# Turning every second step of a prompt attention around: values, scores, transposes

## The chip, the cores and the metric

The kernel runs on one core of a Trainium2 chip. The time is the device time of one execution in microseconds (us). The engines named below are PE (TensorE, matrix products), PEld (its weight loads), ACT (ScalarE), DVE (VectorE), POOL (GpSimd) and SP (SyncE, which issues DMAs). The kernel before takes 1814.83 us, the median of three runs (1814.32 to 1816.25).

## The reference, cut to what matters

One layer of a hybrid decoder is computed for a prompt of 1024 tokens and 32 sample tokens. The part that the change touches is group B of the first sub-layer: causal latent attention of the prompt, with 8 heads, 96 query and key columns and 64 value columns per head.

```python
def masked_attend(q, k, v, q_pos, k_pos):
    s = jnp.einsum('...qhd,...khd->...hqk', q, k).astype(jnp.float32) * (QK_HEAD ** -0.5)
    s = jnp.where(k_pos[None, :] <= q_pos[:, None], s, NEG_INF)
    p = jax.nn.softmax(s, axis=-1).astype(v.dtype)
    return jnp.einsum('...hqk,...khd->...qhd', p, v)
```

Queries, keys and values come from normalised latents by projections (`mla_queries`, `mla_keys_values`). Around it stand a gated chunk mixer, a paged sample attention, an output projection, a memory attention and a gated feed-forward part with a causal convolution; the change leaves their code as it is.

## The kernel before, in words

All is computed in float32, mostly as three products of high and low halves (`mm3`, line 185: high by high, low by high, high by low). The stages follow each other: `phase1` (input projections, mixer), `phase2a` (prompt attention), `phase2b` (sample attention over cached pages), then output projection, memory attention and the feed-forward part.

`phase2a` cuts the attention into 16 units: a head h and a group G of four blocks of 128 queries. A unit with G = 0 (keys 0 to 511) has three steps, one with G = 1 (keys 0 to 1023) four; there are 56 steps, numbered t = 0 to 55 here. `head_unit` gives a unit its parts:

- scores `a(e)` for block e: products into a PSUM tile `s` (two buffers), which DVE moves to `pr` with the mask and the row maximum (lines 1014 and 1018), and the negative maximum `nm` (line 1020);
- exponential `e(e)` on ACT (line 1023), in place on `pr`, with the row sum;
- transposes `T(b)` (line 1031): up to four 128x128 blocks of `pr` into a PSUM tile `tp` (four buffers), which ACT copies to `pth` (line 1033);
- values `V(b)` (line 1046): products of `v` (64 columns, stationary) with `pth`, added up in the PSUM tile `o`. Even query blocks go to partitions 0 to 63 of `o`, odd ones to 64 to 127, so these products use 64 of PE's columns at a time;
- `copy` (line 1053, DVE: `oc<-o`, and a reciprocal) and `out` (line 1059: two transposes of `oc` on PE, then a scaling on DVE, lines 1063).

`head_prep` (line 984, "preps" below) transposes queries and keys of a head; `proj_group` (line 185 with an output named `tp`) makes the projections of later blocks and heads. Both use the `tp` buffers too.

The order of PE, ACT, DVE and POOL in this stage is written out by hand (`manual_schedule`): what a Python loop calls first stands first in each engine's queue. In each step of the loop the parts are called in this order: the low halves left over (`flush`), the transposes of this step with any `out` that is due, the exponentials left over from the step before (`pend`; in the last step of a unit they go ahead of the transposes), the scores of the next unit that `jobs[t]` names, the low halves and sums left over, the values of the step before, and then `extra[t]`, which holds preps, projections, norms and weight sums by a table of steps. From step 32 on, a part `sample()` of the sample attention's preparation goes one stretch further in each step; from step 50 on, so does `mix()`, which squares, scales and transposes the finished part of the output `b_all` (lines 1687, 1693, 1701).

The order of SP, and of the engines outside this stage, is set by a scheduler that the compiler front end runs on costs of its own.

## Time and profile before

| | us |
|---|---|
| median of three runs | 1814.83 (1814.32 to 1816.25) |
| the profiled execution's own time | 1815.49 |
| its span | 1813.8 |
| PE busy | 1791.1 (99%) |
| DVE busy | 1347.4 (74%) |
| ACT busy | 921.0 (51%) |
| POOL busy | 705.9 (39%) |
| prompt attention's steps, in the span | about 203 to 401 |

A row of the timeline tells the start in us from the start of the span, the duration, the engine, the line of the kernel, the operation, output and inputs by the program's names, and what an idle time before it waited for. PE's products are pipelined, so the duration of one overlaps the next; what an instruction costs is read from start to start. The granted clock of PE (PEclk) is a share of full speed. The value products show up in the timeline as two rows for each instruction.

### The profile page before, as it was taken

The page shows a single profiled execution, that of the slowest core. Times are in us where ns is not written, and L with a number is a line of the kernel's source. Part 1 is how long each engine was busy: PE and PEld are TensorE (multiplying, and loading weights), DVE is VectorE, ACT ScalarE, POOL GpSimd, SP SyncE. Part 2 cuts the span into 40 slices and gives each one's busy share as a digit, 9 for nine tenths or more (in the row PEclk, how much of TensorE's full clock was granted, in tenths as well). Part 3 has the DMA queues.
Part 4 walks back from the last instruction along what each step waited for, and adds up shares of the span by engine and source line. Part 5 has one row for each costly group of instructions (what it writes and reads, how often), then busy time and mean ns, then how long its engine had stood idle before and what let it go on. Part 6 is the DMA issues. An engine that isn't in the chain of part 4 may idle for free.

```text
span 1813.8 us, 39386 instructions
## 1 busy us (share of the span) xinstructions
PE 1791.1 (99%) x14259; PEld 1696.6 (94%) x14259; DVE 1347.4 (74%) x2778; ACT 921.0 (51%) x1931; POOL 705.9 (39%) x858
## 2 busy tenths in 40 slices
PE   9999999999999999999999999999999999999999
PEld 8999777769999999998899989999999999999999
DVE  7864777667678777787644678988888888878664
ACT  7335676766556555565434567433333333344442
POOL 1021656534455445453033001476677767400000
PEclk9999999999999999999999999999999999999999
DMA  8101354558876666663655255122222222584242
GB/s 324 48 18 62 118 184 129 164 164 229 226 206 191 190 186 194 178 190 125 188 157 195 97 169 181 58 95 83 72 71 83 72 83 83 163 319 150 88 147 78
DMA packets 153044, 261.06 MB, mean 144 GB/s; under 512 B 20881, under 2 KB 97394, under 8 KB 152850
## 3 DMA queue, kind: packets, MB, share of 16 engines
q1 hardware_dynamic: 151986, 257.50, 45.8%
q8 instruction: 113, 1.85, 0.5%
q10 hardware_dynamic: 864, 1.05, 0.2%
q14 instruction: 81, 0.66, 0.1%
HBM read 212.66 MB, written 45.82 MB: 143 GB/s over the span
## 4 chain that ended last, share of the span: by engine, by line
PE 77%; DVE 5%; ACT 2%; DMA 1%; issue 1%; POOL 1%; SPq 1%; DVEq 0%; ACTq 0%; POOLq 0%
PE s L185 22%; PE d L185 12%; PE b L185 8%; PE E L185 7%; PE F L185 7%; PE X L185 7%; PE A L185 3%; PE o L1046 2%; PE o L1537 2%; PE tp L1031 1%; PE tp L185 1%; PE s L1422 1%; PE tp L984 1%; PE v L185 1%; PE t L185 0%
## 5 line engine op out<-in xcount | busy, mean ns | idle before, releaser
L185 PE MATMUL s<-w2h,ch 128*128 128x256 f32 x1018 | 302.1, 297 | 0.0
L185 PE MATMUL s<-w2h,cl 128*128 128x256 f32 x1018 | 293.6, 288 | 0.0
L185 PE MATMUL s<-w2l,ch 128*128 128x256 f32 x1018 | 293.1, 288 | 0.0
L185 PEld LDWEIGHTS s<-w2h,ch 128*128 128x128 f32 x1018 | 191.6, 188 | 3.3 <-issue 2.9
L185 PEld LDWEIGHTS s<-w2h,cl 128*128 128x128 f32 x1018 | 191.4, 188 | 0.4 <-DVE rqa L257 0.4
L185 PEld LDWEIGHTS s<-w2l,ch 128*128 128x128 f32 x1018 | 191.8, 188 | 0.0
L1458 DVE TENSOR_REDUCE ss<-sq 128x16 f32<-128x1024 f32 x128 | 155.2, 1213 | 29.2 <-ACT sq L1455 29.1
L1407 POOL TENSOR_TENSOR cl<-cT,ch 128x512 fp32r<-128x512 f32 x64 | 86.2, 1346 | 197.8 <-ACT ch L1403 192.0
L1455 ACT ACTIVATE sq<-s 128x512 f32<-128x512 f32 x128 | 76.4, 597 | 72.3 <-PE s L185 72.2
L200 ACT CAST a<-brb 128x528 fp32r<-128x528 f32 x77 | 48.9, 634 | 114.7 <-PE d L185 111.2
L1452 ACT ACTIVATE sq<-s 128x512 f32<-128x512 f32 x128 | 76.6, 599 | 50.4 <-PE s L185 41.2
L201 DVE TENSOR_TENSOR a<-brb,a 128x528 fp32r<-128x528 f32 x77 | 54.3, 706 | 59.1 <-ACT a L200 58.8
L185 PE MATMUL d<-a,w 128*128 128x264 f32 x768 | 95.5, 285 | 1.2 <-DVE G L2366 1.2
L185 PEld LDWEIGHTS d<-a,w 128*128 128x128 f32 x768 | 94.3, 188 | 1.4 <-issue 1.4
L2233 POOL TENSOR_TENSOR lo<-s,hi 128x1024 fp32r<-128x1024 f32 x20 | 64.2, 3208 | 45.7 <-ACT hi L2232 45.7
L2289 ACT COPY a<-A 128x264 f32<-128x264 f32 x43 | 16.1, 375 | 120.6 <-PE A L185 114.3
L185 PE MATMUL mm<-wlo,xh 128*128 128x256 f32 (+3 forms) x272 | 77.1, 286 | 0.1
L185 PE MATMUL mm<-whi,xh 128*128 128x256 f32 (+3 forms) x272 | 77.1, 285 | 0.0
L185 PE MATMUL mm<-whi,xl 128*128 128x256 f32 (+3 forms) x272 | 76.9, 287 | 0.0
L1403 ACT CAST ch<-cT 128x512 fp32r<-128x512 f32 x128 | 73.6, 628 | 0.2 <-issue 0.2
L2355 POOL TENSOR_TENSOR cv<-cv,row 128x1056 f32<-128x1056 f32 x22 | 65.1, 2958 | 21.0 <-ACT cv L2354 21.0
L185 PE MATMUL d<-a,hi 128*128 128x264 f32 x552 | 72.0, 285 | 0.0
(802 smaller groups left out, 6371.3 us busy)
## 6 DMA issues: line engine op xcount, KB each, us to landing
cT<-cT SPq DMA_DIRECT2D x256, 160.0 KB, 2.7
ck<-ck SPq DMA_DIRECT2D x256, 144.0 KB, 3.5
raw<-w_up SPq DMA_DIRECT2D x44, 512.0 KB, 3.6
wsumd<-wsum SPq DMA_DIRECT2D x26, 512.0 KB, 3.5
actd<-cv SPq DMA_DIRECT2D x44, 264.0 KB, 2.4
brb<-actd SPq DMA_DIRECT2D x44, 264.0 KB, 5.6
wsum<-w_down SPq DMA_DIRECT2D x22, 512.0 KB, 3.7
raw<-wsumd SPq DMA_DIRECT2D x20, 512.0 KB, 3.7
```

The lines of the kernel that those rows point to most:

```text
L185: x = self.nc.tensor.matmul(out, l, r, start=first and i == 0, stop=last and i == len(seq) - 1)
L200: first = {"act": nc.scalar.copy, "pool": nc.gpsimd.tensor_copy, "dve": nc.vector.tensor_copy}[eng](hi, src)
L201: low = lambda: nc.vector.tensor_tensor(lo, src, hi, ALU.subtract)
L1046: nc.tensor.matmul(u["o"][g : g + 64, o : o + m * P], s["v"][:, j, h % 4], th[:, z * P : (z + m) * P], start=j == 0, stop=b == len(banks) - 1,
L1403: nc.scalar.copy(d["h"][:, k], src[k])
L1407: (nc.vector if k else nc.gpsimd).tensor_tensor(d["l"][:, k], src[k], d["h"][:, k], ALU.subtract)
L1452: nc.scalar.activation(sq[:, 0], ps[:, :, n0 : n0 + 256], AF.Square)
L1455: nc.scalar.activation(sq[:, 1], pt.rearrange("p (e d) -> p e d", e=2), AF.Square)
L1458: yield lambda: nc.vector.tensor_reduce(s["ss"][:, g0 : g0 + 2].rearrange("p e (z h) -> p z e h", z=2), sq.rearrange("p z e (h d) -> p z e ...
L1537: nc.tensor.matmul(s["o"][j * 32 : j * 32 + 32], S[:, q * 4 + j], d["ck"][:, j, :257], start=q == 0 and j > 0, stop=q == 7)
L2233: eng.tensor_tensor(lo, src, hi, ALU.subtract)
L2355: nc.gpsimd.tensor_tensor(cv, cv, row, ALU.mult)
```

## The change

Only `phase2a` is changed, in two ways.

In the odd steps the parts are called in another order: values of the step before, scores, extras, and at the end this step's transposes. In the even steps the values go from ahead of the extras to the end. So the sequence over two steps, which was transposes, scores, values, extras, and the same again, is now transposes, scores, extras, values (even), values, scores, extras, transposes (odd). The values of steps 1 and 2, of 3 and 4 and so on then stand next to each other, and so do the transposes of steps 1 and 2, 3 and 4.

In the table of extras the preps are entered after the projections, so that within a step the projections follow the scores and the preps come last. No instruction of the stage is added or taken away.

```diff
         put(split_w, (7, 8, 13, 15))
         spread(tok_s, 4, 11)
-        put(preps[1][2:], (3, 4))
-        for h in range(2, 8):
-            b = 7 * (h - 1)
-            put(preps[h], {3: (9, 10, 12, 13), 5: (27, 28, 34, 35), 6: (32, 33, 41, 42), 7: (39, 38, 44, 45)}.get(h, (b, b + 1, b + 3, b + 4)))
-        extra[2][:0] = preps[0][2:]
         spread(late[0][0], 11, 21)
...
         spread(late[2][0], 24, 30)
+        put(preps[0][2:], (2, 2))
+        put(preps[1][2:], (3, 4))
+        for h in range(2, 8):
+            b = 7 * (h - 1)
+            put(preps[h], {3: (9, 10, 12, 13), 5: (27, 28, 34, 35), 6: (32, 33, 41, 42), 7: (39, 38, 44, 45)}.get(h, (b, b + 1, b + 3, b + 4)))
...
                     self.flush()
+                    turn = [lambda b=b: u["T"](b) for b in banks] + outs.pop(t, [])
+                    values, V = V, [lambda u=u, b=b: u["V"](b) for b in banks]
                     if k == len(u["steps"]) - 1:
                         for f in pend:
                             f()
                         pend = []
-                    for b in banks:
-                        u["T"](b)
-                    for f in outs.pop(t, []):
+                    for f in values if t % 2 else turn:
                         f()
                     for f in pend:
                         f()
...
                     self.flush()
                     self.flush_sums()
-                    for f in V:
-                        f()
-                    V = [lambda u=u, b=b: u["V"](b) for b in banks]
...
                     for f in extra[t]:
                         f()
-                    t += 1
-                    if t == 32:
+                    if t == 31:
                         steps.append(sample())
                     steps = [x for x in steps if next(x, 0) is None]
+                    for f in turn if t % 2 else values:
+                        f()
+                    t += 1
```

Two places show what this does to the engines' queues. The first is PE around the last step (t = 30) of the unit h = 4, G = 0. Before, from the last score product of step 29 on (`s`), with values (`o<-pth`), transposes (`tp<-ident,pr`) and the two transposes of `out` (`tp<-ident,oc`):

```order
L185 MATMUL s_4406<-kTh_3977,qTl_4169 128x512
L1046 MATMUL o_4412<-pth_4339,v_2698 64x256 x2
L1031 MATMUL tp_4423<-ident_60,pr_749_4154 128x128
L1031 MATMUL tp_4423<-ident_60,pr_766_4233 128x128
L1059 MATMUL tp_4428<-ident_60,oc_4395 128x128 x2
L1046 MATMUL o_4412<-pth_4389,v_2698 64x128 x2
L1046 MATMUL o_4412<-pth_4389,v_2698 64x256
L1031 MATMUL tp_4443<-ident_60,pr_778_4275 128x128
```

And now, in the same place:

```order
L185 MATMUL s_4399<-kTh_3978,qTl_4183 128x512
L1030 MATMUL tp_4412<-ident_60,pr_766_4233 128x128
L1030 MATMUL tp_4412<-ident_60,pr_745_4142 128x128
L1030 MATMUL tp_4412<-ident_60,pr_736_4097 128x128
L1030 MATMUL tp_4412<-ident_60,pr_766_4233 128x128
L1030 MATMUL tp_4423<-ident_60,pr_745_4142 128x128
L1030 MATMUL tp_4423<-ident_60,pr_766_4233 128x128
L1058 MATMUL tp_4428<-ident_60,oc_4419 128x128 x2
L1045 MATMUL o_4388<-pth_4413,v_2698 64x128 x2
L1045 MATMUL o_4388<-pth_4413,v_2698 64x256
L1045 MATMUL o_4388<-pth_4424,v_2698 64x128 x2
L185 MATMUL s_4448<-kTh_4317,qTh_4377 128x128
```

The four transposes of step 29 have moved behind its scores, and the values of step 30 (`pth_4424`), which stood behind the next step's transposes and scores, now follow those of step 29 at once. In ACT's queue the copy to `pth_4424` stands behind the exponential over 1024 keys of the next unit, as it did before:

```order
L1022 ACTIVATE pr_793_4347,rsum_4274<-pr_793_4347,nm_4348,rq_2427 128x896
L1032 COPY pth_4413<-tp_4412 128x512
L1022 ACTIVATE pr_804_4392,rsum_4274<-pr_804_4392,nm_4393,rq_2427 128x1024
L1032 COPY pth_4424<-tp_4423 128x256
L1032 COPY pth_4490<-tp_4489 128x512
```

The second place is ACT at the end of the stage (from step 51 on). Before, the small copy of step 51's transposes (`pth_5533`) stood ahead of three squares of `mix()` (k, q), and two scalings of `b_all` behind that of step 55 (`pth_5624`):

```order
L1023 ACTIVATE pr_1039_5509,rsum_5425<-pr_1039_5509,nm_5510,rq_2427 128x1024
L1033 COPY pth_5533<-tp_5532 128x256
L1687 ACTIVATE k_5527,mixr_5529<-b_all_2409 128x512
L1687 ACTIVATE q_5528,mixr_5529<-b_all_2409 128x512 x2
L1033 COPY pth_5546<-tp_5545 128x512
L1033 COPY pth_5553<-tp_5552 128x512
L1033 COPY pth_5577<-tp_5576 128x512
L1033 COPY pth_5584<-tp_5583 128x512
L1033 COPY pth_5599<-tp_5598 128x512
L1033 COPY pth_5606<-tp_5605 128x512
L1693 ACTIVATE b_all_2409<-b_all_2409,mixr_5529 128x512 x2
L1033 COPY pth_5624<-tp_5623 128x256
```

Now both small copies stand behind `mix()`:

```order
L1022 ACTIVATE pr_1039_5509,rsum_5423<-pr_1039_5509,nm_5510,rq_2427 128x1024
L1686 ACTIVATE k_5523,mixr_5525<-b_all_2409 128x512
L1686 ACTIVATE q_5524,mixr_5525<-b_all_2409 128x512 x2
L1032 COPY pth_5541<-tp_5540 128x256
L1032 COPY pth_5546<-tp_5545 128x512
L1032 COPY pth_5553<-tp_5552 128x512
L1032 COPY pth_5582<-tp_5581 128x512
L1032 COPY pth_5589<-tp_5588 128x512
L1032 COPY pth_5599<-tp_5598 128x512
L1032 COPY pth_5606<-tp_5605 128x512
L1692 ACTIVATE b_all_2409<-b_all_2409,mixr_5525 128x512 x4
L1032 COPY pth_5631<-tp_5630 128x256
```

The copy of step 51 has moved behind the three squares, and the copy of step 55 behind all four scalings. On PE the values that need these two copies stand ahead of the transposes of step 53 and of `mix()`'s own transposes. Counted in PE's queue, the value products form 55 runs without another kind of product between them before, and 29 now. Outside the stage only SP's weight-sum transfers and some rows of the feed-forward part change places with a neighbour.

## The prediction

> **What bounds the kernel now.** I read the page first: PE is busy all through, so only what shortens PE's own work, or its waits, can show.

> ```profile
> PE 1791.1 (99%) x14259; PEld 1696.6 (94%) x14259; DVE 1347.4 (74%) x2778; ACT 921.0 (51%) x1931; POOL 705.9 (39%) x858
> ```

> Then the stage by itself (windows of the steps, of one stretch near their start, and of their end), who made PE wait in it, and one group of DVE's:

> ```profile
> 203.00:398.00 195.00, 186.47 (x1271) 138.44 (x1271) 132.21 (x455) 137.58 (x351) 100.77 (x151) 0.98 0.49 154
> 212.24:215.65 3.41, 2.03 (x9) 1.31 (x10) 2.15 (x5) 1.64 (x4) 0.94 (x2) 1.00 0.41 104
> 215.65:222.47 6.82, 6.82 (x26) 5.20 (x25) 4.03 (x15) 0.96 (x2) 3.10 (x5) 0.50 0.59 199
> ...
> PE tp L1031 <- ACT pr L1023: 3.0, 5, 1.1
> PE s L185 <- DVE pr L1018: 2.2, 7, 1.3
> PE tp L1031 <- DVE qTl L207: 1.1, 1, 1.1
> PE s L185 <- ACT qTh L204: 1.0, 1, 1.0
> ...
> L1053 DVE COPY oc<-o 128x256 f32<-128x256 f32 x15 | 6.2, 410 | 0.0
> ```

> After the stretch's length the columns are the busy time of PE, PEld, DVE, ACT and POOL, then the granted clock, the DMA share and GB/s. PE works 186.5 of 195 us; ACT and DVE have about 60 us to spare, but not everywhere: the waits are short and sit where ACT's exponentials or DVE's moves are late. In 215.65 to 222.47 the granted clock is 0.50, after 3.41 us in which PE was busy for 2.03 only.

> **What a run of values costs.** The timeline of PE at one step:

> ```profile
> 282.57 0.39 PE L185 MATMUL s<-kTl,qTh 96*128 96x512 f32 x1
> 282.80 0.39 PE L185 MATMUL s<-kTh,qTl 96*128 96x512 f32 x1
> 283.12 1.08 PE L1046 MATMUL o<-pth,v 128*64 128x256 f32 x8
> 284.13 0.38 PE L185 MATMUL tp<-w2h,ckh 128*128 128x256 f32 x1
> 284.36 0.28 PE L185 MATMUL tp<-w2l,ckh 128*128 128x256 f32 x1
> 284.48 0.28 PE L185 MATMUL tp<-w2h,ckl 128*128 128x256 f32 x1
> ...
> 289.05 0.66 PE L1031 MATMUL tp<-ident,pr 128*128 128x128 f32 x4
> 289.46 0.46 PE L185 MATMUL s<-kTh,qTh 96*128 96x448 f32 x1
> 289.75 0.37 PE L185 MATMUL s<-kTl,qTh 96*128 96x448 f32 x1
> 289.97 0.36 PE L185 MATMUL s<-kTh,qTl 96*128 96x448 f32 x1
> ```

> A score product takes 0.23 from start to start (282.57 to 282.80), so the values could start at 283.03; they start at 283.12, 0.09 late. Their eight rows take 1.01; the four such rows at 323.10 below take 0.58, so four rows are worth 0.43 and each run has 0.15 on top. The product behind them takes 0.23 where its neighbour takes 0.12: another 0.11; a transpose behind them loses about 0.06 (below, two at 323.68 and three at 325.06 are busy for 0.44 and 0.55, so one is 0.11, but the two take 0.28). So a run costs 0.09 + 0.15 + 0.06 to 0.11 = 0.30 to 0.35 us beside its work. Transposes between scores cost next to nothing: four and the first score product take 0.70 (289.05 to 289.75), and by themselves 4 x 0.11 + 0.22. Standing together gains nothing for them, nor does moving preps behind projections.

> The last two steps already have their values together, and show that the price is paid once:

> ```profile
> 387.19 1.08 PE L1046 MATMUL o<-pth,v 128*64 128x256 f32 x8
> 388.57 1.30 PE L1046 MATMUL o<-pth,v 128*64 128x256 f32 x10
> 389.80 0.55 PE L1031 MATMUL tp<-ident,pr 128*128 128x128 f32 x3
> ...
> 391.53 0.44 PE L1046 MATMUL o<-pth,v 128*64 128x128 f32 x4
> 391.90 1.09 PE L1031 MATMUL tp<-ident,pr 128*128 128x128 f32 x8
> 393.56 1.14 PE L1046 MATMUL o<-pth,v 128*64 128x256 f32 x8 [0.56 <-ACT pth L1033]
> 396.04 1.08 PE L1046 MATMUL o<-pth,v 128*64 128x256 f32 x8
> 397.42 1.52 PE L1046 MATMUL o<-pth,v 128*64 128x256 f32 x14
> 398.87 1.53 PE L1701 MATMUL tp<-ident,b_all 128*128 128x128 f32 x12
> 401.42 0.39 PE L1422 MATMUL s<-bd,krq 128*128 128x128 f32 x2
> ```

> Ten rows take 1.23 and four 0.37 (388.57, 391.53), together 1.60; the fourteen at 397.42 take 1.45.

> **The gain.** 26 runs fewer, at 0.09 + 0.15, are 6.2 us. What follows a run changes too: before 11 runs had a product of line 185 behind them and 44 something like a transpose (11 x 0.11 + 44 x 0.06 = 3.9); now about 23 and 6 (2.9). What scores pay behind values stands in no row; I take the 0.11 of the projection, the same kind of product, and between 0.06 and 0.16 the term moves by 1.1 either way. Sum 7.2 us, 0.28 for each pair. It counts only where PE does not wait. Nine pairs stand ahead of a wait that ACT or DVE ends: step 3 (the wait for qTh), 17, 23 (the 1.1 for qTl), 31, 41, 47, and three at the end. The other 17 give 17 x 0.28 = 4.8.

> **The price: values that now follow too soon.** Where a unit's last step is even and brings no scores, both values follow the scores of the step before almost at once. At step 30 the trace of before shows what they then wait for:

> ```profile
> 323.10 0.65 PE L1046 MATMUL o<-pth,v 128*64 128x256 f32 x4
> 323.68 0.44 PE L1031 MATMUL tp<-ident,pr 128*128 128x128 f32 x2
> 323.96 0.38 PE L1059 MATMUL tp<-ident,oc 128*128 128x128 f32 x2
> 324.27 0.86 PE L1046 MATMUL o<-pth,v 128*64 128x128 f32 x6
> 325.06 0.55 PE L1031 MATMUL tp<-ident,pr 128*128 128x128 f32 x3
> 325.93 0.77 PE L1031 MATMUL tp<-ident,pr 128*128 128x128 f32 x5 [0.32 <-ACT pr L1023]
> ...
> 324.55 1.24 ACT L1023 ACTIVATE pr<-pr,nm,rq 128x1024 f32<-128x1024 f32 x1 [0.97 <-DVE nm L1020]
> 325.79 0.35 ACT L1033 COPY pth<-tp 128x256 f32<-128x256 f32 x1
> ```

> The scores end at 323.10; the small copy is done at 326.14, 3.04 later. Before, its values came long after it. Now PE has four transposes (0.44), two more (0.22), `out` (0.31), and the values of step 29 (0.09 + 0.64, the six rows at 324.27 less 0.15) to do, 1.7 us, and then waits 1.3 for step 30's, less about 0.4 because the DVE copy to `oc` (410 ns) now stands behind the maximum. The 0.32 of before goes. So 0.6 is lost here. Behind the waiting values stand the next unit's scores, and with them DVE. Steps 16 and 40 have the same shape with projections or sample work between, and ACT has more ahead of the copy; I take 0.5 each. Sum 1.6; bounds 0 (if ACT is early) and 3.9 (three full waits of 1.3).

> **The price at the end.** ACT's rows there:

> ```profile
> 390.69 0.35 ACT L1033 COPY pth<-tp 128x256 f32<-128x256 f32 x1
> 390.94 0.63 ACT L1687 ACTIVATE k<-b_all 128x512 f32<-128x512 f32 x1
> 392.94 2.03 ACT L1033 COPY pth<-tp 128x512 f32<-128x512 f32 x4
> ```

> Without the small copy the squares run from 390.69 to 392.69, and the copy of step 51 is done at about 393.0. PE finishes step 52's transposes at 391.3 and has nothing ahead of these values: it waits 1.7 where it waited 0.56 before. Step 52's values need the second large copy (394.0) and end at 394.6; sixteen transposes and `out` follow to 396.6 (before, this point was 396.04), then eighteen value rows to 398.8. Meanwhile ACT has its last large copy out at 397.5, scales `b_all` four times (four operations of the squares' size at 0.63 are 2.5) and copies step 55 at 400.4. PE's last values and 12 transposes then start at 400.4 and 400.9; before, the 12 started at 398.87. That is 2.0 late; each pair gained before it brings all of it forward a little, so I take +1.5, with bounds of 0 and 2.5.

> **Sum.** -4.8 + 1.6 + 1.5 = -1.7 on the profiled execution's 1815.49, which is 1813.8. The three runs' median is 0.7 below that execution, part of which may be the slow clock near the start, so I forecast 1813.6. About 0.2% (3.6 us) is what a measurement of this kernel can tell from no change: under 1811.2 is faster, over 1818.5 slower.

> **Rivals.** *The waits are covered and the gain stays.* ACT has 57 us to spare in the stage; if its order happens to be early at steps 16, 30 and 40, and the tail costs nothing, 1814.8 - 7.2 = 1807.6; with half of the prices about 1810. The half clock near the start may go too: values instead of transposes now stand ahead of the wait for qTh, filling its window better, and 6.82 us at 0.50 are worth up to 3.4. Against it: the orders shown above put those copies behind long ACT work. Chance 0.27.

> *The pauses halve the clock.* At the end PE would be idle from about 389.7 to 390.7 and 391.3 to 393.0 in one window of 3.41 us, less busy than the 2.03 of 3.41 that came ahead of the half clock at 215.65. Then 6.82 us at 0.50 cost up to 3.4: 1817.0. If the pause at step 30 does the same, 1820.4, on the other side; it decides from two such drops on, or one and full waits at 16, 30 and 40. Against it: windows elsewhere in this stage have waits of 1.1 to 1.3 us without a drop. Chance of over 1818.5: 0.15. [...]

> *A run of two steps pays twice*, because its second half goes to another tile `o`. Then nothing is won and the prices stay: 1814.8 + 3.1 = 1817.9. The fourteen rows at 397.42 stay in one tile, so they do not rule it out. [...] Chance 0.05, within 0.2%.

> **Chances and range.** The forecast has 0.53 (its own range 1811.5 to 1817, from the bounds of the prices). Faster 0.27, within 0.2% 0.58, slower 0.15. The range takes in half of the first rival's case, and the second's with one drop: 1809.5 to 1818.5.

> **What would show it.** In the profile of the changed kernel: runs of values followed by scores, the first score product about 0.1 long; waits of values (line 1045) for the copy (line 1032) of 0.5 to 2 us near steps 16, 30, 40 and 52, where there was one of 0.56; the sample attention's first product (L1422) 1 to 3 us ahead of 401.42. It is wrong if values do not wait there, if the scores behind values cost far more than 0.11, or if the granted clock has more or fewer stretches at 0.50 in the stage.

## The result, and the profile after

The changed kernel takes 1824.67 us, the median of six runs (1821.92 to 1827.14), against 1815.49 (1814.32 to 1818.50) for six runs of the kernel before on the same chip: a ratio of 1.0051 (95% interval 1.0040 to 1.0061). It is slower, by about 9 us. The forecast was 1813.6 with a range up to 1818.5.

The profiled execution took 1824.68, its span 1823.0. From the page, and from the windows and PE's waits of the changed kernel, from 203 us to the sample attention's first product at 409.27 (before: 401.42):

```profile
PE 1790.2 (98%) x14259; PEld 1704.6 (94%) x14259; DVE 1348.4 (74%) x2778; ACT 919.9 (50%) x1931; POOL 706.4 (39%) x858
```

```profile
203.00:409.27 206.27, 189.82 (x1297) 149.48 (x1296) 132.82 (x460) 139.38 (x357) 102.68 (x154) 0.96 0.46 146
353.53:356.95 3.42, 1.46 (x11) 1.05 (x12) 3.24 (x14) 3.08 (x9) 1.99 (x3) 1.00 0.56 167
356.95:363.77 6.82, 6.82 (x37) 5.60 (x36) 4.21 (x14) 1.42 (x5) 4.06 (x6) 0.50 0.68 224
394.50:397.91 3.41, 1.30 (x10) 0.83 (x8) 0.13 (x1) 3.38 (x11) 0.00 (x0) 1.00 0.00 0
397.91:401.32 3.41, 3.26 (x16) 1.94 (x17) 2.10 (x13) 1.07 (x3) 0.00 (x0) 0.50 0.00 0
```

```profile
PE tp L1058 <- DVE rsum L1053: 3.3, 4, 1.6
PE tp L1030 <- ACT pr L1022: 3.1, 4, 1.2
PE tp L1030 <- DVE qTl L207: 2.9, 3, 1.4
PE o L1045 <- ACT pth L1032: 2.3, 2, 1.5
PE s L185 <- DVE pr L1017: 2.0, 7, 1.1
```

The same window and waits of the kernel before, up to 401.42:

```profile
203.00:401.42 198.42, 189.55 (x1298) 140.99 (x1296) 134.06 (x460) 140.20 (x357) 102.01 (x153) 0.98 0.48 151
```

```profile
PE tp L1059 <- DVE rsum L1054: 0.3, 1, 0.3
```

PE is idle for 206.27 - 189.82 = 16.45 us, before 198.42 - 189.55 = 8.87. Its waits for `rsum`, that is `out` waiting for DVE, went from 0.3 to 3.3; for `qTl` from 1.1 to 2.9; values for ACT's copy from 0.6 to 2.3. And the clock is at 0.50 in two stretches more, each behind a window in which PE was busy for less than half.

**An account of the stage.** For each profile I took the 1296 PE instructions (fewer or more where a kernel leaves out or adds some) up to the sample attention's first product. Idle time is the sum of the gaps before them; half clock is half of PE's busy time inside the stretches at 0.50; work is the rest. A pause that the duration of the instruction before still covers counts as work.

| | stage | idle | half clock | work |
|---|---|---|---|---|
| before | 198.5 | 8.9 | 3.4 | 186.3 |
| before, two further profiles | 198.3 / 200.0 | 8.7 / 10.0 | 3.4 / 3.4 | 186.2 / 186.6 |
| changed | 206.4 | 16.4 | 8.5 | 181.5 |
| changed, a further profile | 208.9 | 18.6 | 8.5 | 181.7 |

So the change takes 4.8 us of work off PE, adds 7.6 us of waiting, and loses 5.1 us more to the clock: 7.9 us. Split by kind of instruction, from start to start, the 4.8 are 6.4 less for values, scores, projections and preps, and 1.6 more for the transposes of `pr` and `oc`. Another 1.1 us is lost at the start of the sample attention, where a product of `cl` now waits for DVE:

```profile
PE s L1448 <- DVE cl L1406: 1.1, 1, 1.1
```

**Where it happens.** Instruction by instruction the changed kernel is mostly within 2 us of the one before from 220 to 353 us: saved work and new waits cancel. Between 353 and 360 it falls back by more than 5 us. PE and DVE around step 40:

```profile
353.68 0.87 PE L1030 MATMUL tp<-ident,pr 128*128 128x128 f32 x6 [0.96 <-DVE qTl L207]
356.12 0.41 PE L1058 MATMUL tp<-ident,oc 128*128 128x128 f32 x2 [1.57 <-DVE rsum L1053]
356.78 0.91 PE L1127 MATMUL tp<-ident,qr 32*128 32x32 f32 x8 [0.24 <-DVE kTl L201]
357.62 0.70 PE L1045 MATMUL o<-pth,v 128*64 128x128 f32 x4
```

```profile
354.64 0.75 DVE L1013 CUSTOM_DVE_ANT_0 pr<-s,cmask,nm 128x512 f32<-128x512 f32 x1
355.31 0.08 DVE L1013 DVE_READ_ACCUMULATOR2_ANT nm<- 128x1 f32 x1
355.43 0.21 DVE L1019 TENSOR_SCALAR nm<-nm,rq 128x1 f32<-128x1 f32 x1
355.56 0.41 DVE L1052 COPY oc<-o 128x256 f32<-128x256 f32 x1
355.89 0.17 DVE L1053 RECIPROCAL rsum<-rsum 128x4 f32<-128x4 f32 x1
```

Step 37 is the last of its unit and odd. Its `copy` is due two steps later, in step 39, which is odd: it is now called at that step's end, behind the score moves. Its `out` is due in step 40, which is even: at that step's start. The two have become neighbours. PE reaches `out` while DVE still moves scores, and waits 1.57 us; before, a whole step lay between. With the 0.96 ahead of it this leaves PE busy for 1.46 of 3.42 us, and 6.82 us at half clock follow.

The second loss, 4.2 us by instruction, is at the end:

```profile
395.82 0.77 PE L1030 MATMUL tp<-ident,pr 128*128 128x128 f32 x5 [0.79 <-ACT pr L1022]
398.06 2.46 PE L1045 MATMUL o<-pth,v 128*64 128x128 f32 x12 [1.47 <-ACT pth L1032]
400.46 2.37 PE L1030 MATMUL tp<-ident,pr 128*128 128x128 f32 x16
```

```profile
396.29 0.61 ACT L1686 ACTIVATE q<-b_all 128x512 f32<-128x512 f32 x1
396.81 0.19 ACT L1686 ACTIVATION_READ_ACCUMULATOR q<-b_all 128x1 f32 x1
397.03 0.63 ACT L1686 ACTIVATE q<-b_all 128x512 f32<-128x512 f32 x1
397.56 0.19 ACT L1686 ACTIVATION_READ_ACCUMULATOR q<-b_all 128x1 f32 x1
397.66 1.32 ACT L1032 COPY pth<-tp 128x256 f32<-128x256 f32 x3
```

The values wait for the copy behind the mixer's squares, as forecast, for 1.47 us; with the 0.79 before it that again leaves a window less than half busy (1.30 of 3.41), and the twelve value rows behind it and the first of the sixteen transposes run at half clock.

**What the change does give.** The values of steps 27 and 28, which go to two tiles `o`, now together, with the score product behind them:

```profile
321.23 0.87 PE L1045 MATMUL o<-pth,v 128*64 128x128 f32 x8
322.03 0.50 PE L185 MATMUL s<-kTh,qTh 96*128 96x512 f32 x1
```

Before, step 27's four rows stood here, and step 28's four at 323.10 (shown in the prediction):

```profile
319.61 0.44 PE L1046 MATMUL o<-pth,v 128*64 128x128 f32 x4
319.98 0.64 PE L984 MATMUL tp<-ident,q 128*96 128x128 f32 x4
```

Eight rows take 0.80 us from 321.23 to 322.03; before, the same eight took 0.37 and 0.58 in two places. A run that goes on in another tile `o` pays its 0.15 once. At step 30 this gain is lost:

```profile
325.43 0.41 PE L1058 MATMUL tp<-ident,oc 128*128 128x128 f32 x2 [1.08 <-DVE rsum L1053]
325.77 1.30 PE L1045 MATMUL o<-pth,v 128*64 128x128 f32 x10
327.00 0.33 PE L185 MATMUL s<-kTh,qTh 96*128 96x128 f32 x1
```

The ten rows of steps 29 and 30 take 1.23, where six and four took 0.79 and 0.37 before (at 324.27 and 327.32). ACT's copy for the last four ends at 326.58, and they start at 326.63: part of the 1.23 is a short wait.

### The profile page after: what moved, and what is told of

It is laid out like the page before. It is cut to its first block, busy times and chain, and to the rows that moved or that the text cites. A ratio compares the mean times of both kernels' runs of the same rounds, so it can differ in the third digit from the quotient of the medians.

```text
span 1823.0 us, 39392 instructions
## 1 busy us (share of the span) xinstructions
PE 1790.2 (98%) x14259; PEld 1704.6 (94%) x14259; DVE 1348.4 (74%) x2778; ACT 919.9 (50%) x1931; POOL 706.4 (39%) x858
## 4 chain that ended last, share of the span: by engine, by line
PE 75%; DVE 7%; ACT 3%; issue 2%; DMA 1%; POOL 1%; SPq 0%; DVEq 0%; ACTq 0%
PE s L185 22%; PE d L185 12%; PE b L185 7%; PE E L185 7%; PE X L185 7%; PE F L185 7%; PE A L185 3%; PE o L1045 2%; PE o L1536 2%; PE tp L1030 1%; PE tp L185 1%; PE s L1421 1%; DVE ss L1457 1%; PE v L185 1%; ACT pr L1022 1%
## 5 line engine op out<-in xcount | busy, mean ns | idle before, releaser
L185 PE MATMUL s<-w2h,ch 128*128 128x256 f32 x1018 | 302.2, 297 | 0.0
L185 PE MATMUL s<-w2h,cl 128*128 128x256 f32 x1018 | 293.9, 289 | 0.0
L185 PE MATMUL s<-w2l,ch 128*128 128x256 f32 x1018 | 293.4, 288 | 0.0
L185 PEld LDWEIGHTS s<-w2h,ch 128*128 128x128 f32 x1018 | 191.8, 188 | 3.2 <-issue 2.9
L185 PEld LDWEIGHTS s<-w2h,cl 128*128 128x128 f32 x1018 | 191.6, 188 | 0.5 <-DVE rqa L257 0.4
L185 PEld LDWEIGHTS s<-w2l,ch 128*128 128x128 f32 x1018 | 191.9, 189 | 0.0
L185 PE MATMUL d<-a,w 128*128 128x264 f32 x768 | 95.4, 285 | 1.1 <-DVE G L2365 1.1
L185 PEld LDWEIGHTS d<-a,w 128*128 128x128 f32 x768 | 94.3, 189 | 1.3 <-issue 1.3
L185 PE MATMUL mm<-wlo,xh 128*128 128x256 f32 (+3 forms) x272 | 77.2, 286 | 0.1
L185 PE MATMUL mm<-whi,xh 128*128 128x256 f32 (+3 forms) x272 | 77.2, 285 | 0.0
L185 PE MATMUL mm<-whi,xl 128*128 128x256 f32 (+3 forms) x272 | 77.0, 287 | 0.0
L2288 ACT COPY a<-A 128x264 f32<-128x264 f32 x43 | 16.1, 374 | 120.6 <-PE A L185 113.3
L185 PE MATMUL d<-a,hi 128*128 128x264 f32 x552 | 72.0, 285 | 0.0
```

The source lines that it names most:

```text
L185: x = self.nc.tensor.matmul(out, l, r, start=first and i == 0, stop=last and i == len(seq) - 1)
```

## The experiments

All are edits of the two kernels. "Idle", "half clock" and "work" are those of the account above, in the one profiled execution of each run. The longest pauses that carry a verdict are quoted; the numbers are gathered here.

| run | ratio to before (95%) | stage | idle | half clock | work |
|---|---|---|---|---|---|
| e1_outs_start | 1.0065 (1.0052 to 1.0078) | 209.2 | 20.2 | 8.9 | 180.1 |
| e2_tail_before | 1.0039 (1.0026 to 1.0052) | 204.5 | 14.2 | 8.5 | 181.7 |
| e3_filled (34 more) | 1.0037 (1.0024 to 1.0050) | 205.3 | 14.8 | 5.1 | 185.4 |
| e5_turn_only | 1.0041 (1.0029 to 1.0053) | 206.9 | 16.1 | 10.0 | 180.9 |
| e6_values_only | 1.0035 (1.0024 to 1.0046) | 205.0 | 18.3 | 7.7 | 179.0 |
| e7_values_chosen | 1.0003 (0.9993 to 1.0012) | 200.1 | 12.7 | 6.8 | 180.6 |
| e8_outs_start_sample | 1.0048 (1.0035 to 1.0061) | 210.3 | 19.0 | 10.2 | 181.1 |
| e9_values_chosen_table | 0.9998 (0.9987 to 1.0009) | 197.4 | 13.8 | 1.7 | 181.9 |
| e10_before_filled (30 more) | 1.0003 (0.9994 to 1.0012) | 196.5 | 5.9 | 0.0 | 190.6 |
| e11_outs_start_cos | 1.0023 (1.0014 to 1.0033) | 199.7 | 15.5 | 3.4 | 180.7 |
| e12_chosen_filled (38 more) | 0.9996 (0.9987 to 1.0005) | 199.3 | 11.0 | 1.7 | 186.6 |
| e13_all_filled (61 more) | 1.0034 (1.0021 to 1.0046) | 201.8 | 11.4 | 1.7 | 188.7 |
| e14_before_less (32 fewer) | 1.0008 (0.9999 to 1.0017) | 198.6 | 11.8 | 6.8 | 180.0 |

**Does `out` wait because it follows its copy too closely?** The copy and `out` go back to the step's start:

```diff
-turn = [lambda b=b: u["T"](b) for b in banks] + outs.pop(t, [])
+turn, done = [lambda b=b: u["T"](b) for b in banks], outs.pop(t, [])
-for f in values if t % 2 else turn:
+for f in (values if t % 2 else turn) + done:
```

> The changed kernel, but the copy of o and the transposes of out stand near the start of every step, behind its transposes (even) or values (odd), so that a whole step lies between a unit's copy and its out. Theory A (out waits for DVE because in units with an odd last step copy and out became neighbours): the three waits of out for line 1053's reciprocal, 3.0 us together, go, and with the pause at 356.1 us the half clock at 357 to 364, which cost 3.4; about 6.4 us less than the changed kernel, +2.8 against the kernel before (ratio 1.0015). Theory B (my prediction's step: the copy behind the row maximum helps, the values then wait instead): no gain, ratio 1.004 to 1.006, new waits of values for ACT's copies at steps 30 and 40.

The time did not fall, yet the places say more than the time. At step 40 the wait of 1.57 is gone (0.46 is left, for another reason) and no half clock follows: there theory A holds. At step 30 the wait only changed its name. The timeline of PE in this run:

```profile
325.63 0.38 PE L1058 MATMUL tp<-ident,oc 128*128 128x128 f32 x2
326.31 0.86 PE L1045 MATMUL o<-pth,v 128*64 128x128 f32 x6 [0.29 <-ACT pth L1032]
328.47 0.44 PE L1045 MATMUL o<-pth,v 128*64 128x128 f32 x4 [1.29 <-ACT pth L1032]
```

`out` no longer waits, so the values reach ACT's small copy early and wait 1.29: theory B, the prediction's own mechanism, at the 1.3 of its working. What ate the gain was new. DVE's queue at 378.76, behind it the copy, the scores and PE's `out`:

```profile
378.76 0.75 DVE L1173 TENSOR_SCALAR cosT<-cosT,cols 128x1024 f32<-128x1024 f32 x1 [4.15 <-DMA cosT<-c_cosT]
```

```profile
376.24:379.65 3.41, 1.17 (x10) 0.57 (x9) 0.89 (x2) 0.47 (x2) 1.45 (x2) 1.00 0.78 298
379.65:389.89 10.24, 7.87 (x33) 6.03 (x34) 5.24 (x18) 3.77 (x7) 0.00 (x0) 0.50 0.62 186
```

DVE waited 4.15 us for the load of `cosT`, PE 3.24 in turn, and 10.24 us at half clock followed. SP issued that load at 373.82, behind one more pair of weight-sum transfers than in the kernel before (366.40 there); that queue's order is a scheduler's. The changed kernel has that pair in front of the load too (issued at 371.78): DVE did not wait for it in the first profile, but 2.1 us in the further one, with 3.41 us at half clock behind it at 384.7. Two runs tested this, both with `copy` and `out` at the step's start. The first starts the sample preparation a step earlier (`if t == 30`), the second puts the scaling of `cosT`, and what follows it in `sample()`, two steps later (two more `yield`).

> The run with copy and out at the step's start, but the parts of the sample attention's preparation begin one step earlier, so that the load of cosT is issued about 3.5 us earlier. Theory A (in that run DVE waited 4.15 us for cosT, with out and the scores behind it, and the pause halved the clock for 10.2 us at 380): no wait for cosT, no stretch at 0.50 near 380; about 3.2 + 5.1 us less than that run, ratio 1.0015 to 1.0025. Rival (the wait at 380 comes from out itself): ratio 1.005 to 1.007 as there.

> The run with copy and out at the step's start, and DVE's scaling of cosT two steps later, so that nothing on DVE stands behind the load of cosT. Theory A (that run lost its gain at 380 us to that load, which is issued on the queue of SP after a pair of weight-sum transfers): no pause of 3.2 at 380 and no half clock there, 6 to 7 us less than that run, ratio 1.002 to 1.003. Rival (out itself waits): ratio 1.005 to 1.007.

The first missed: the load was issued only 1.7 us earlier (372.16), DVE came to it earlier still and waited 5.28, and PE 3.52. In this run 3.41 us at half clock also stood at 357.15, behind waits of 0.46 and 0.80 around step 40. The second came out as theory A expects: ratio 1.0023, no stretch at 0.50 from 376 to 391, PE busy for 13.41 of these 15 us. So the neighbours `copy` and `out` cost the changed kernel about 5 us (1.0051 against 1.0023, of which the later scaling of `cosT` may have a share), much of it through the clock, and the load of `cosT` stood ready as the next limit. Of the 5.1 us by which this profile loses less to the clock, 1.7 are not theirs: the two waits at the end were as long as in the changed kernel (0.77 and 1.47), but no half clock followed them.

**The end, and the table of extras.** One run leaves the steps from 48 on in the old order (`odd = t % 2 and t < 48`), one puts the table of extras back and keeps the turned steps.

> The changed kernel, with the steps from 48 on in the order of the kernel before. Theory A (the end lost 3.2 us through the waits at 395.8 and 398.1 and the half clock behind them, and the sample attention started 1.1 late because of it): 3 to 4 us less than the changed kernel, +5 to +6 against the kernel before (ratio 1.003), no stretch at 0.50 near 398. Theory C (the half clock there comes by its own count, whatever the waits): about 1.5 less, ratio 1.004, the stretch stays.

> The changed kernel with the table of extras in the order of before (preps ahead of the projections of their step): only the turned steps are left of the change. If the waits of transposes for DVE's low half qTl (2.9 us, before 1.1) come from preps that stand last, next to the transposes: 1 to 2 us of waits go, and the half clock at 357, whose window holds one of them (0.96), may go with them (3.4): ratio 1.002 to 1.0045. If the table is without effect: ratio 1.005, waits for qTl as in the changed kernel.

With the old end nothing more is lost after 390 us than in the kernel before (waits of 0.49 and 0.56), neither the two longer waits nor the stretch at 398 nor the 1.1 at the start of the sample attention: theory A in its places. The ratio is 1.0039, some 2 us less than the changed kernel where 3 to 4 were expected; the intervals of the two overlap. The table shows no clear effect: at 1.0041 the interval overlaps that of the changed kernel, and the waits for `qTl` stay at 2.8. With the transposes back at the start of every step (e6_values_only below) these waits fall to 1.1, as in the kernel before: they belong to the turned transposes.

**Does the clock fall because of the pauses?** Transposes of the identity, which nobody reads, ahead of `out` at steps 30 and 40 (`for _ in range(fill)`, 9 and 13), and step 52's last transpose 12 times more; then the same in more pauses of the changed kernel, where `cosT` is also scaled two steps later, and in five pauses of the kernel before.

> The changed kernel, with transposes that nobody reads in the three longest pauses of PE: 9 and 13 ahead of the transposes of out at steps 30 and 40 (1.0 and 1.4 us), 12 behind the transposes of step 52 (1.3 us). The pauses keep their length, but PE works in them. Theory A (the clock falls after a window of 3.41 us that is about half idle): the stretches at 0.50 at 357 to 364 and 398 to 401 go, 5.1 us less than the changed kernel, +4 against the kernel before (ratio 1.0023). Theory C (the drops do not hang on these pauses): same time as the changed kernel or slower, ratio 1.005, stretches still there or elsewhere.

> The changed kernel with transposes that nobody reads in seven pauses (the three of the earlier run, and ahead of transposes at steps 0, 48 and 52 and of the first scores of head 0's upper queries), and with DVE's scaling of cosT two steps later. Theory A (of the changed kernel's 9 us, 8.5 are the clock's, less 3.4 of before; the waits took 7.6 and the values gave 4.8): the times come near the kernel before, ratio 0.999 to 1.001. Rival C: ratio 1.004 to 1.006 as the changed kernel.

> The kernel before, with 30 transposes that nobody reads in five of PE's pauses that were there before the change (7 ahead of the last transpose of step 0, 8 ahead of the first scores of the unit of head 0 and the upper queries, 2, 9 and 4 ahead of transposes at steps 31, 48 and 52). Theory A (a window of 3.41 us with a pause in it halves the clock): the half clock between 203 and 223 us, worth 1.7 to 5.1 in nearly all profiles so far, goes, and the kernel is about 3.4 us faster: ratio 0.998, the longest times go too. Rival C (the clock falls by its own count): ratio 1.000 to 1.001, the stretch stays.

In e3_filled both stretches are gone, as theory A says; the two windows around step 40, here from 350.69 to 357.51, now keep a clock of 1.00. A new stretch of 3.41 stands at 381.42, behind a pause for `cosT`:

```profile
350.69:354.10 3.41, 1.93 (x15) 1.49 (x13) 2.04 (x6) 3.41 (x11) 2.62 (x4) 1.00 0.47 137
354.10:357.51 3.41, 3.08 (x31) 2.74 (x32) 2.71 (x11) 1.87 (x4) 2.10 (x3) 1.00 0.58 203
378.01:381.42 3.41, 1.05 (x8) 0.81 (x9) 2.14 (x6) 1.59 (x3) 0.00 (x0) 1.00 0.81 250
381.42:384.83 3.41, 3.41 (x18) 2.89 (x18) 1.50 (x7) 1.17 (x2) 0.00 (x0) 0.50 0.61 180
```

With all filled the stage loses only 1.7 to the clock, and yet the ratio is 1.0034 where I expected about 1. In the kernel before the stage loses nothing to the clock any more, but the time stays the same. One reason that the account shows is that filling is not free: 30 transposes add 4.3 us of work (0.14 each) and take away 3.0 of idle time, 61 add 7.2 and take away 5 (with the later `cosT` in it). In e10_before_filled the stage is still 2.0 us shorter; a stretch of 6.83 at 883.5 us, outside the stage, took that back in its profile, and why the median gains nothing is not shown. The times that I expected of the last two were too low by about 6 and 4 us. As to the stretches themselves: all four profiles with the pause of step 40 unfilled and `out` next to its copy have one there (changed, its further profile, e2_tail_before, e5_turn_only), and neither filled one does. At the end four of the six profiles with the unfilled pauses and the changed order have one, e1_outs_start and e11_outs_start_cos have none. So the pauses are shown to be the cause, and at the end a cause that does not act in every execution.

Further profiles of the kernels as they are show the same thing from the other side.

> The kernel before once more, for its granted clock. Theory A (windows of 3.41 us that lie by chance): stretches at 0.50 at the same weak places (205 to 216, 870) or missing there, and none at 357 or 398; time 1810.5 plus 1.7 or 3.4 for each stretch.

> As the last: the kernel before, another profile; the same is expected.

> The changed kernel once more. Theory A: stretches at 0.50 again at 357 and near 398, since the windows there are over half idle wherever they lie, and one at 205 to 220; rival C: at other places.

The kernel before had 6.83 us at 215.7 in one (1812.33 us in all, with 3.41 at 847) and 3.41 at 233.7 and 288.4 in the other (1817.51, with 3.41 at 872): the weak places change, none at 357 or near 400. The second profile's place at 288 was not among those I had named. The times do not fit what I expected of them either: both profiles have 10.24 us at 0.50, and are 5.2 us apart. The changed kernel lost its clock at 357 and 402 again, and at 384.7 as well:

```profile
354.01:357.42 3.41, 1.59 (x19) 1.15 (x18) 2.92 (x12) 2.60 (x7) 1.55 (x3) 1.00 0.86 298
357.42:360.83 3.41, 3.41 (x18) 2.54 (x14) 2.49 (x10) 0.00 (x0) 1.89 (x3) 0.50 0.53 165
398.38:401.79 3.41, 1.89 (x16) 0.77 (x15) 1.67 (x11) 2.56 (x7) 0.00 (x0) 1.00 0.00 0
401.79:405.20 3.41, 3.41 (x18) 3.40 (x17) 0.55 (x3) 1.76 (x3) 0.12 (x1) 0.50 0.00 0
```

**Is a better order hidden in it?** Only the values are turned, and transposes and `out` stay at the start of every step; then only where no wait was known to follow; and that with the old table; and at last with the old table and filled pauses, and steps 2 and 20 left as before too. The edit of the second of these runs (the first has no "middle"):

```diff
+at = "middle" if t - t % 2 in (16, 30, 40) or t >= 48 else "start" if t % 2 else "end"
-for f in values if t % 2 else turn:
+for f in (values if at == "start" else []) + turn:
...
+for f in values if at == "middle" else []:
+    f()
 for f in extra[t]:
...
-for f in turn if t % 2 else values:
+for f in values if at == "end" else []:
```

> Only the values are turned: those of step t-1 stand at the end of an even step t, those of step t at the start of step t+1, ahead of its transposes; the transposes and out stand at the start of every step as in the kernel before. Theory A (the waits came in with the turned transposes and out, which follow too closely on DVE's work; the runs of values gain about 4.8 us): the waits for rsum (3.0) and the two new ones for qTl (1.5) go; what is left is the values that wait for ACT's copy at steps 30 and 40 and at the end, 1.3 to 1.5 each. Ratio 0.998 to 1.001, up to 1.003 if one of these waits halves the clock. Rival D (standing together gains nothing, a run that changes its tile pays twice): PE's work as before, ratio 1.001 to 1.004.

> As the run with the values alone turned, but around steps 16, 30 and 40 and from step 48 on the values stand in the place that they had before, behind the scores. Theory A: no new wait is left and the gain of about 19 pairs at 0.19 to 0.28 stays, 3.6 to 5.3 us less than the kernel before, less what vanishes in waits that were there before: ratio 0.9975 to 0.9985. Rival D (no gain from standing together): ratio 0.9995 to 1.001.

> The run with chosen values turned, and the table of extras in the order of the kernel before. If the table is without effect here as it was with the turned steps: the same ratio as that run within 0.0007. If preps that stand last are harmful ahead of transposes at the start of the next step: 1 to 2 us less.

> Chosen values turned with the table of before, step 2 left as before too, and 38 transposes that nobody reads in five of PE's pauses. Theory A: the half clock near 215 and 376 goes and PE's work is about 4 us less, of which 1 to 2 are left beside the new waits: ratio 0.997. If the pairs' gain is all turned into waits: the ratio of the kernel before with filled pauses, 0.998. Rival C (the clock does not hang on the pauses): 1.000.

With all values turned, those of step 30 and of the end wait 1.77 and 1.58 us as theory A says, but the time is above its range: DVE again waits for `cosT` (2.82), PE behind it, and 6.83 us at half clock follow at 378. The chosen values end where the kernel before stands: 1.0003, 0.9998, 0.9996, all three intervals holding 1. Rival D has the time right and the reason wrong, since PE's work is less by 5.7 and 4.4 us in the first two of them (and by 7.3 in e6_values_only). Theory A had the work right and the time wrong: the gain has turned into waits (4.9 us more idle in e9_values_chosen_table), and in e7_values_chosen into 3.8 us of waits and 3.4 of half clock. PE's waits in e9_values_chosen_table:

```profile
PE tp L1033 <- ACT pr L1025: 4.9, 6, 1.9
PE s L185 <- DVE pr L1020: 3.2, 7, 1.4
PE tp L1033 <- DVE qTl L207: 1.9, 2, 1.5
```

Before these were 3.0, 2.2 and 1.1, as the prediction quotes.

**Would any work taken from PE show here?** The order is left as it was, and 32 value products of 256 columns are left out:

```diff
 for j, e, z, m in runs:
+    if j and e % 2 and m == 2 and b in ((1, 3, 4) if G else (1,)):
+        continue
```

> The kernel before, in its old order, with 32 value products of 256 columns left out (the odd query blocks of some key blocks, so those values are not added up), 4 or fewer in each unit: at 0.215 us each 6.9 us less work for PE, at the places where the change takes work away. Theory P (PE's own work bounds the stage; the new order is at fault): nearly all of it shows, 5 to 6.5 us less, ratio 0.9965 to 0.9973. Theory E (DVE and ACT pace the stage as closely; waits take up most of what PE gains): 1 to 3 us less, ratio 0.9984 to 0.9995, with longer waits for DVE's moves and ACT's exponentials.

The answer is no. PE's work is 6.3 us less, its idle time 2.9 more, and the ratio is 1.0008, short even of theory E. Waits and the stretch behind them:

```profile
PE tp L1031 <- ACT pr L1023: 4.8, 6, 1.5
PE s L185 <- DVE pr L1018: 2.3, 7, 1.2
PE tp L1031 <- DVE qTl L207: 1.8, 2, 1.5
```

```profile
294.67:298.09 3.42, 1.78 (x13) 1.17 (x12) 3.24 (x11) 1.65 (x4) 3.27 (x4) 1.00 0.00 0
298.09:304.92 6.83, 6.77 (x31) 5.85 (x32) 2.66 (x12) 2.60 (x6) 4.32 (x6) 0.50 0.37 110
```

Theory P falls: the old order does not let a gain through either. In this profile waits take up about half of what PE saves, and one stretch of 6.83 at half clock, behind a wait for `qTl` that was 1.1 before and is 1.5 now, gives back the other 3.4. How often that stretch comes in the other executions is not shown; it stays open whether the clock alone keeps the median from falling. That the rest of the program swallows what the stage gains is not seen: what follows the sample attention's first product, less its half clock, takes 1408.2 to 1412.9 us in the 18 profiles, with no trend by when it starts (398.7 to 412.4).

## Why the prediction was wrong, point by point

Its sum was -1.7 and the profiled execution shows +9.2, a miss of 10.9. By size, two steps failed in the changed kernel: the place of the copy to `oc`, counted as a gain of 0.4 at step 30 and in truth 3.0 us of new waits, and the clock, put at nothing and worth 5.1. By terms, against what its working implies for idle time (2.4 us of gain lost in waits that existed, plus prices of 3.1):

- **Runs of values.** Forecast 7.2 us of PE's work, measured 4.8. The mechanism was right: the price is paid once for two steps, also across a change of the tile `o` (eight rows of steps 27 and 28 take 0.80 us, before 0.37 and 0.58), so the third rival falls. The price was nearly right as well: values, scores, projections and preps gave 6.4. What it lacked is a term for the moved transposes: "Standing together gains nothing for them" put them at nothing, and they took 1.6 more, perhaps in short waits that the account cannot see. With the transposes left in place (e6_values_only) the work fell by 7.3.
- **"It counts only where PE does not wait ... The other 17 give 17 x 0.28 = 4.8."** This step would have failed even without the new waits. Places without a visible wait were taken as places where PE alone sets the time. With chosen values turned, 4.4 to 5.7 us less work left a ratio of 1.0003 and 0.9998; with 32 products left out in the old order, 6.3 us less left 1.0008. I had written that the spare 60 us of ACT and DVE are "not everywhere", and yet counted 17 of the pairs in full.
- **"less about 0.4 because the DVE copy to `oc` (410 ns) now stands behind the maximum".** Counted as a gain, it was the missed price. The copy came next to its own `out`, and PE waited for it at steps 30 and 40 (1.08 and 1.57) and two shorter times, 3.3 us in all against 0.3. Step 40 lost 1.57 to it and 3.4 to the half clock behind it, more than all prices that I had put down (3.1); the 0.96 for `qTl` in the same window had its part in the clock's share.
- **Values too soon at steps 16, 30 and 40, 1.6 us.** In the changed kernel they hardly waited, since `out` had waited in their place. With `out` out of the way the wait was 1.29 at step 30, against the 1.3 of the working.
- **The end, +1.5.** The wait was there (1.47, where I had 1.7, and 0.85 more for step 55's copy), but the loss was 4.2 us: these waits, a half clock of 3.41 us behind the first, and 1.1 at the start of the sample attention. Of idle time the whole stage got 7.6 instead of the 5.5 implied.
- **The clock.** Forecast nothing, with 0.15 for the rival; it took 5.1 us. The rival named the place at the end rightly and step 30 instead of step 40. Its evidence against, "windows elsewhere in this stage have waits of 1.1 to 1.3 us without a drop", was weak: in the table at the end 17 of 18 windows busy for less than 0.5 are followed by 0.50, and 13 of over 8200 busy for more than 0.8. The share of the whole window tells them apart, so pauses add up (0.96 and 1.57 ahead of the half clock at 356.95), and where the window lies decides which of them fall together.
- The working put the moved preps at nothing, and no run shows otherwise (e5_turn_only).

2.4 + 2.1 + 5.1 + 1.1 are 10.7 of the 10.9.

## What to carry to other kernels

Before reordering to save a few us on the busiest engine, leave out as much of its work at the same places and time that: if nothing shows (here 6.3 us less work gave a ratio of 1.0008), a better order of that engine alone is not likely to show either, and the waits and the granted clock of that run tell what takes the gain. Where steps are turned around, look at every pair of a producer on one engine and a consumer on another that lie on two sides of a step's boundary; turning can make neighbours of them (here `out` then waited 1.57 us for its copy at step 40). And price a pause of TensorE twice: for its length, and for what the clock may do behind it if the pauses in one window of 3.41 us add up to about half of it (here 34 of 50 windows busy for less than 0.6 were followed by half clock).

## What the runs showed of the hardware

| busy share of the window | windows | followed by 0.50 |
|---|---|---|
| under 0.5 | 18 | 17 |
| 0.5 to 0.6 | 32 | 17 |
| 0.6 to 0.8 | 150 | 14 |
| over 0.8 | over 8200 | 13, all near 870 us |

So a window that is about half idle is often enough: 34 of the 50 that were busy for less than 0.6 were followed by 0.50, among them the 2.03 of 3.41 us ahead of 215.65 in the kernel before. And the same pauses may or may not bring it: the waits at the end (0.79 and 1.47, 0.77 and 1.47) did in the changed kernel and did not in e11_outs_start_cos. The clock is only a part of the 8 us by which executions of the kernel before differ (1811.1 to 1819.2 in one series of 29): its three profiles all have 10.24 us at 0.50, and took 1812.33, 1815.49 and 1817.51. Where the rest comes from is open. Why the clock falls near 870 us behind windows that are full (3.41 of 3.41 us from 867.60 in the kernel before, then 3.41 at 0.50) is not explained either.

A window full of transposes brought no drop: in the changed kernel PE was busy for 3.31 of the 3.41 us from 333.06, from 333.28 on with transposes alone, and the next window, from 336.48, kept a clock of 1.00. Nor was any half clock left where step 40's pause was filled with transposes (1.00 from 350.69 to 357.51 in e3_filled).
